# Gate products and pairs of short latent products in a fixed alternation, and the second rotary pair beside the latent heads: a two-layer encoder on one core

## The chip, the cores and the metric

The kernel runs on one core of one Trainium2 chip. The core has TensorE (PE in the profile, its weight loads PEld), VectorE (DVE), ScalarE (ACT), GpSimd (POOL) and SyncE (SP, which here issues nearly all loads), each with a queue of its own that it works through in order. The metric is the device time of one execution in microseconds (us), as the median of the runs shown.

## The reference

A bidirectional encoder of two layers over 256 tokens of width 2048, in float32. What matters here is the token mixer of each layer:

```python
h = rmsnorm(x, g_mix[i])
z = h @ w_in[i]
dq, dk, dv, cq, ckv, kr, ga, gb = jnp.split(z, split_at, axis=-1)
...
od = diff_attention(dq, dk, dv, lam)            # 8 heads, two softmax maps each
y_diff = od.reshape(b, s, DIFF_WIDTH) @ w_branch_diff[i]
qf = (rmsnorm(cq, g_q_latent[i]) @ w_q_up[i]).reshape(b, s, MLA_HEADS, MLA_NOPE_DIM + MLA_ROPE_DIM)
q_nope = qf[..., :MLA_NOPE_DIM]
q_rope = apply_rope(qf[..., MLA_NOPE_DIM:], cos_m, sin_m)
...
om = latent_attention(q_nope, q_rope, k_nope, k_rope, v_mla)   # 8 heads
y_mla = om.reshape(b, s, MLA_WIDTH) @ w_branch_mla[i]
merged = jax.nn.sigmoid(ga) * y_diff + jax.nn.sigmoid(gb) * y_mla
x = x + merged @ w_out[i]
```

A feed-forward part and a gated embedding follow in each layer; the change does not touch them.

## The kernel before

Activations are kept transposed, features on the 128 partitions and the 256 tokens along the free axis. Every operand of a product is a float32 value split into a high and a low part in a rounded format. Weights arrive in pieces of 128x1024 (512 KB). For each piece, SP issues the load into one of four w32 buffers (line 203), ACT copies it to the high part whi (line 204, three buffers) and DVE subtracts to get the low part wlo (lines 204 and 82, three buffers). This is `piece`; in this text the DVE subtraction is called the weight split.

A piece holds eight 128x128 tiles. `emit` spends two matmuls on each tile: whi against the activation's high and low part, 512 columns (line 254), and wlo against the high part, 256 columns (line 255). They go into one of four PSUM banks of the pool ps_mm, named mm. `joined` then adds the two halves of a bank: ACT copies one half to SBUF (line 279), DVE adds the other (line 82). That addition frees the bank.

Three kinds of product matter here. A *gate* (`gate`, line 632) has 16 tiles and so two pieces; its joined sum is multiplied by a row of norm factors and stored. A *plain pair* is `queries_up(n)` with n of 0, 2, 4 or 6: one piece of w_q_up makes two short products of four tiles each, one for each of two heads, and each is joined and split into high and low part again. A *rotary pair* is `queries_up(8)` or `queries_up(10)`: the same two short products, and then `rotated` turns each: a shuffle, two multiplications and an addition on DVE, then two half-height copies on ACT and two half-height splits on DVE for each product. queries_up(8) serves latent heads 0 to 3, queries_up(10) serves heads 4 to 7.

In each layer the eight heads of the differential attention run first, two steps of the generator `beside` in each head. `beside` makes the queries and keys of later heads, the latent keys (`keys_up`), the shared rotary key (`shared_key`, matmuls on line 409), and last the four pairs queries_up(8), (0), (2), (10) and four gates. After them come the values of the latent heads (`values`, w_v, lines 223 to 227), then the eight latent heads. Each latent head calls `some_gate` twice. That makes one gate, and ahead of it what the dictionary `later` names for that step: the normalisation and transposes of four differential heads (`settle`, transposes on line 693), queries_up(4) and queries_up(6). In between stand scores (line 437), transposes of the softmax weights (line 459) and the heads' outputs (lines 674 and 747).

The order of instructions on each engine is not that of the source alone. A scheduler orders them when the program is built, by its own times for them; `tc.issue_after` and `tc.add_manual_dep` with NO_SYNC force an order between two instructions without a wait. Engines wait for one another through semaphores.

Of the kernel before, what the change touches and what calls it, by code (L numbers as in the profile page):

```python
# [49 lines left out]
NO_SYNC = mybir.DependencyInfo(mybir.DependencyClass.NoSync, mybir.DependencyReason.DATA)  # L50
# [10 lines left out]
def encoder(ctx, tc, x, p, positions, cols, lams, wq, wk, wv, wcq, wckv, wkr, wga, wgb,  # L61
            w_q_up, w_kn, w_v, w_bd, w_bm, w_out, w_gate, w_up, w_down, w_pin, w_pg, w_pin_end, w_pg_end, g_end, rope_c, out):
    nc = tc.nc
    V, A, PE = nc.vector, nc.scalar, nc.tensor
# [13 lines left out]
    def bank(ps=ps_at, tag="at", name="at", shape=(P, 2 * T)):  # L78
        return ps.tile(list(shape), F32, tag=tag, name=name)

    def tt(o, a, b, op):
        return V.tensor_tensor(out=o, in0=a, in1=b, op=op)  # L82
# [17 lines left out]
    def operand(t):  # L100
        return t.rearrange("p c t -> p (c t)")
# [4 lines left out]
    def in_turn(u):  # L106
        return u.rearrange("p (c h t) -> p h t c", c=2, h=2)
# [21 lines left out]
    ones = const.tile([P, P], F32, name="ones")  # L129
# [103 lines left out]
            if j:  # L233
                tt(sq0[0], sq0[0], sq0[j], ALU.add)

    last_split, last_mm, chores, sq0, step, last_block = [], [], [], [], [], [None]

    def after_splits():

# [5 lines left out]
    def emit(acc, hi, lo, at, us, first, last, whole):  # L245
        for j, u in enumerate(us):
            s, start, stop = slice((at + j) * P, (at + j + 1) * P), first and j == 0, last and j == len(us) - 1
            t = in_turn(u)
            if whole:
                PE.matmul(acc[:, :T], hi[:, s], t[:, 0], start=start, stop=False)  # L250
                PE.matmul(acc[:, :T], hi[:, s], t[:, 1], start=False, stop=False)
                PE.matmul(acc[:, :T], lo[:, s], t[:, 0], start=False, stop=stop)
            else:
                PE.matmul(acc, hi[:, s], t, start=start, stop=False)  # L254
                last_block[0] = PE.matmul(acc[:, T:], lo[:, s], t[:, 0], start=False, stop=stop)  # L255

    def product(src, us, whole=False):
# [10 lines left out]
    def pair(src, us):  # L268

        n = len(us)  # L270
        hi, lo = piece(src.rearrange("n p m -> p n m"), 2 * n)
        for j in range(2):
            acc = bank(ps_mm, "mm", "mm")
            emit(acc, hi, lo, j * n, us, True, True, False)
            yield acc

    def joined(acc, o=None):
        t = scratch("join", 3)
        A.activation(t, acc[:, T:], AF.Copy)  # L279
        o = scratch("a", 4) if o is None else o  # L280
        tt(o, acc[:, :T], t, ALU.add)
        return o

    def split(u, src, gain=None, blocks=False):
        src = src.rearrange("p (c t) -> p c t", c=2) if blocks else by_parity(src)
        hi, lo = (parts(u)[:, j] for j in range(2))
        if gain is None:
            return A.activation(hi, src, AF.Copy), tt(lo, src, hi.bitcast(F32), ALU.subtract)  # L288
        return A.activation(hi, src, AF.Copy, scale=gain), stt(lo, src, gain, hi.bitcast(F32), ALU.mult, ALU.subtract)  # L289
# [96 lines left out]
    def rotated(a, c_, s_, o):  # L386
        turn(a, c_, s_)
        for j, q in enumerate(stacked(o)):
            own, other = (slice(64 * i, 64 * i + 64) for i in (j, 1 - j))
            A.activation(q[own], by_parity(a[own]), AF.Copy, scale=MLA_SCALE)  # L390
            stt(q[other], by_parity(a[own]), MLA_SCALE, q[own].bitcast(F32), ALU.mult, ALU.subtract)
# [4 lines left out]
    def shared_key(src, us, c_, s_):  # L396

        acc = bank(ps_mm, "mm", "mm")
        half = NC // 2
        for k in range(0, NC, half):  # L400
            w = wts.tile([P, PT * P], F32, tag="w32", name="wk32", bufs=W_BUFS)[:, : half * 64]
            both = wts.tile([P, PT * P], F32R, tag="whi", name="wkey", bufs=3)
            hi, lo = both.rearrange("p (k c n) -> p c k n", c=2, n=64)[:, 0], both.rearrange("p (k c n) -> p c k n", c=2, n=64)[:, 1]
            nc.sync.dma_start(w, src[:, k * 64 : (k + half) * 64])
            w = w.rearrange("p (k n) -> p k n", n=64)
            A.activation(hi, w, AF.Copy)
            tt(lo, w, hi.bitcast(F32), ALU.subtract)
            for j in range(half):
                PE.matmul(acc, both[:, j * P : (j + 1) * P], in_turn(us[k + j]), start=k + j == 0, stop=k + j == NC - 1)  # L409
        a, low = scratch("a", 4), slice(0, 64)  # L410
        base = acc[low, :T]
        for part in (acc[64:, :T], acc[low, T:]):
            t = scratch("join", 3)
            A.activation(t[low], part, AF.Copy)
            tt(a[low], base, t[low], ALU.add)
            base = a[low]
        A.activation(a[64:], a[low], AF.Copy)
        turn(a, c_, s_)
        for j, t in enumerate(krs):
            hi, lo = (parts(t)[:, i] for i in range(2))  # L420
            own = slice(64 * j, 64 * j + 64)
            A.activation(hi, by_parity(a), AF.Copy)
            tt(lo[own], by_parity(a[own]), hi[own].bitcast(F32), ALU.subtract)
# [103 lines left out]
    for L in range(DEPTH):  # L527
# [31 lines left out]
        def queries_keys(h):  # L559
            for which, w in enumerate((wq, wk)):  # L560
                a = joined(product(w[L, h], ua))
                sh = scratch("sh", 2)
                V.stream_shuffle(sh, a, ROPE16)
                tt(sh, sh, sr, ALU.mult)
                tt(a, a, cr, ALU.mult)
                tt(a, a, sh, ALU.add)
                split(qk[h][which], a, None if which else DIFF_SCALE)
# [17 lines left out]
        def keys_up(n):  # L585
            for acc in pair(w_kn[L, n : n + 2], ckv):
                kn.append(operand(fb(len(kn), F32R)))
                split(kn[-1], joined(acc))

        def queries_up(n):  # L590
            for acc in list(pair(w_q_up[L, n : n + 2], cq)):
                if n < MH:
                    qn.append(operand(fa(PLACES[len(qn)], F32R)))
                    split(qn[-1], joined(acc), MLA_SCALE)
                else:
                    if n > MH:
                        qr.append(operand(fc(len(qr) - 2, F32R)))
                    at = qr[len(qr) - 1] if n > MH else qr[ropes[0]]
                    rotated(joined(acc), cos_m, sin_m, at)
                    ropes[0] += 1  # L600
# [13 lines left out]
        def beside():  # L614

            for h in range(2, DH):
                queries_keys(h)
                yield
                if h < 6:
                    keys_up(2 * h - 4)  # L620
                elif h == 7:
                    shared_key(wkr[L], ua, crm, srm)
                yield
            for j, n in enumerate((8, 0, 2, 10)):
                queries_up(n)
                if j % 2:
                    gate(wga, gate_a, next(todo))
                yield
            for _ in range(2):
                gate(wga, gate_a, next(todo))  # L630

        def gate(w, store, n):
            tt(store(n), joined(product(w[L, n], ua)), R, ALU.mult)
# [12 lines left out]
        todo = iter(range(NC))  # L646
# [38 lines left out]
        def settle(h0):  # L685

            rd = rsqrt(ssd[:, 2 * h0 : 2 * h0 + 8], P, SUB_EPS, 8)
            for h in range(h0, h0 + 4):
                t = bank()
                for b in range(2):  # L690
                    o, j = od[h][:, b * P : (b + 1) * P], 2 * (h - h0) + b
                    ts(o, o, rd[:, j : j + 1], None, ALU.mult)
                    PE.transpose(t[:, b * P : (b + 1) * P], o, ident)  # L693
                split(ods[h], t[:, :T], gsub[:, L : L + 1], blocks=True)
# [17 lines left out]

        oms = ub[12:] + ub[8:12]
        ahead = iter(range(EARLY))
        later = {0: lambda: settle(0), 2: lambda: queries_up(4), 4: lambda: settle(4), 7: lambda: queries_up(6)}
        steps = itertools.count()

        def some_gate():
# [49 lines left out]
        acc, add = stream(ub, f"g_ffn{L}")  # L768
# [5 lines left out]
        R, _, pre = normed_rows(acc, lambda: product(w_gate[L, 0], ub), lambda: product(w_up[L, 0], ub))  # L774
# [5 lines left out]
        for part, (f0, f1) in enumerate(FF_PARTS):  # L780
            for f in range(f0, f1):
                a = pre.pop(0) if pre else joined(product(w_gate[L, f], ub))
                tt(a, a, R, ALU.mult)
                s = scratch("sig", 2)
# [7 lines left out]
            if last:  # L792
                acc, add = stream(ub, f"g_ple{L}")
# [8 lines left out]
            if part == 1 and L == DEPTH - 1:  # L802
# [7 lines left out]
                hi, lo = piece(w_pin_end, 8)  # L810
                for b in range(2):
                    acc_ = bank(ps_mm, "mm", "mmv")
                    for k in range(2):
                        s = slice(k * 512, (k + 1) * 512)
# [14 lines left out]
        else:  # L829
            acc, add = stream(ua, f"g_mix{L + 1}")  # L830
        for n in range(FM if final else NC):
            a = pre.pop(0) if pre else joined(product(w_pg[L * NC + n], ub))
            tt(a, a, R, ALU.mult)
            s = scratch("sig", 2)
# [4 lines left out]
            if final and n in (3, 5):  # L839
                b = (n - 3) // 2  # L840
                t = bank()
# [6 lines left out]
    for a in range(0, first, 2):  # L848
        m = min(2, first - a)
        hi, lo = piece(w_pg_end[:, a * 512 : (a + m) * 512], 4 * m)  # L850
        for j in range(m):
            s = slice(j * 512, (j + 1) * 512)
# [176 lines left out]
```

## Time and profile before

| what | value |
|---|---|
| runs | 2720.01, 2720.53 and 2720.7 us, median 2720.53 |
| the profiled execution's own time | 2720.81 us |
| its span, first to last instruction | 2719.0 us |
| granted TensorE clock, mean | 0.999 |
| share of the span on the chain that ended last | PE 98%, DVE 1% |
| ACT's weight copies (line 204) | x1024, 1030 ns each |
| DVE's weight splits (line 82, wlo) | x1024, 1189 ns each |
| SP's queue, share of 16 DMA engines | 60.5% |

Matmuls are pipelined and their ends are modelled, so the time that one takes from the engine is read from the distance of the starts of two neighbours, not from its duration. The same holds for DVE, where one instruction's end lies beside the next one's start. A row of the timeline gives the start, the duration, the engine, the line, the operation, output and inputs by their names, their shape and the number of instructions, and behind them in brackets the engine's idle time before it with what ended it. A row of the table by stretch gives the stretch and its length, then the busy time of PE, PEld, DVE, ACT and POOL, the granted clock, the share of the DMA engines that was busy and GB/s. The two layers run the same stages: the stretch that the change touches lies from about 184 to 330 us in layer 0 and from about 1534 to 1680 in layer 1.

### The profile page before, as it was taken

The page shows a single profiled execution, that of the slowest core. Times are in us where ns is not written, and L with a number is a line of the kernel's source. Part 1 is how long each engine was busy: PE and PEld are TensorE (multiplying, and loading weights), DVE is VectorE, ACT ScalarE, POOL GpSimd, SP SyncE. Part 2 cuts the span into 40 slices and gives each one's busy share as a digit, 9 for nine tenths or more (in the row PEclk, how much of TensorE's full clock was granted, in tenths as well). Part 3 has the DMA queues.
Part 4 walks back from the last instruction along what each step waited for, and adds up shares of the span by engine and source line. Part 5 has one row for each costly group of instructions (what it writes and reads, how often), then busy time and mean ns, then how long its engine had stood idle before and what let it go on. Part 6 is the DMA issues. An engine that isn't in the chain of part 4 may idle for free.

```text
span 2719.0 us, 43648 instructions
## 1 busy us (share of the span) xinstructions
PE 2706.3 (100%) x16608; PEld 2482.9 (91%) x16608; DVE 2064.6 (76%) x3426; ACT 1570.1 (58%) x2562; POOL 1.7 (0%) x9
## 2 busy tenths in 40 slices
PE   9999999999999999999999999999999999999998
PEld 8999999999999999999989899999999999999997
DVE  8899668777667777777869986687776677677777
ACT  7786557565445545555747865565554455455555
POOL 0000000000000000000000000000000000000000
PEclk9999999999999999999999999999999999999999
DMA  7555566666666666666665555666656666666665
GB/s 253 178 166 180 164 201 200 201 200 201 197 205 201 194 201 209 201 203 199 202 200 172 164 180 173 201 201 201 201 200 197 205 202 190 212 200 201 200 199 164
DMA packets 157058, 531.53 MB, mean 195 GB/s; under 512 B 17200, under 2 KB 23472, under 8 KB 156848
## 3 DMA queue, kind: packets, MB, share of 16 engines
q1 hardware_dynamic: 156272, 527.90, 60.5%
q8 instruction: 130, 2.13, 0.3%
q10 hardware_dynamic: 576, 0.85, 0.1%
q14 instruction: 80, 0.66, 0.1%
HBM read 526.58 MB, written 2.10 MB: 194 GB/s over the span
## 4 chain that ended last, share of the span: by engine, by line
PE 98%; DVE 1%; ACT 0%; issue 0%; DMA 0%; SPq 0%; ACTq 0%
PE mm L254 61%; PE mm L255 30%; PE mmv L223 1%; PE mmv L227 1%; PE mmv L226 1%; PE S L437 1%; PE at L459 1%; PE at L674 0%; PE at L747 0%; DVE wlo L82 0%; DVE a L82 0%; DMA w<-in_wv 0%; ACT whi L204 0%; PE at L693 0%; PE mm L409 0%
## 5 line engine op out<-in xcount | busy, mean ns | idle before, releaser
L204 ACT ACTIVATE whi<-w 128x1024 fp32r<-128x1024 f32 (+2 forms) x1024 | 1054.5, 1030 | 1070.0 <-issue 512.5
L82 DVE TENSOR_TENSOR wlo<-w,whi 128x1024 fp32r<-128x1024 f32 (+2 forms) x1024 | 1217.4, 1189 | 574.3 <-ACT whi L204 563.7
L254 PE MATMUL mm<-ub,whi 128*128 128x512 f32 x3904 | 1281.4, 382 | 3.2 <-DVE a L82 3.2
L254 PE MATMUL mm<-ua,whi 128*128 128x512 f32 x3704 | 1222.1, 383 | 0.0
L255 PE MATMUL mm<-ub,wlo 128*128 128x256 f32 x3904 | 1063.2, 273 | 0.0
L255 PE MATMUL mm<-ua,wlo 128*128 128x256 f32 x3704 | 1010.6, 273 | 0.0
L254 PEld LDWEIGHTS mm<-ub,whi 128*128 128x128 f32 x3904 | 737.6, 189 | 105.8 <-DVE a L82 3.8
L254 PEld LDWEIGHTS mm<-ua,whi 128*128 128x128 f32 x3704 | 699.6, 189 | 94.7
L255 PEld LDWEIGHTS mm<-ub,wlo 128*128 128x128 f32 x3904 | 749.5, 192 | 0.4
L255 PEld LDWEIGHTS mm<-ua,wlo 128*128 128x128 f32 x3704 | 711.0, 192 | 2.2 <-DVE wlo L82 0.6
L82 DVE TENSOR_TENSOR a<-mm,join 128x256 f32<-128x256 f32 x418 | 173.8, 417 | 0.1
L279 ACT ACTIVATE join<-mm 128x256 f32<-128x256 f32 x444 | 162.8, 368 | 4.2 <-PE mm L255 4.0
L82 DVE TENSOR_TENSOR xT<-xT,mm 128x256 f32<-128x256 f32 x256 | 106.8, 420 | 33.4 <-PE mm L255 29.3
L82 DVE TENSOR_TENSOR a<-a,row 128x256 f32<-128x256 f32 x204 | 86.1, 424 | 5.8
L288 ACT ACTIVATE ua<-a 128x256 fp32r<-128x256 f32 x120 | 59.1, 492 | 2.6 <-DVE a L82 2.6
L82 DVE TENSOR_TENSOR ua<-a,ua 128x256 fp32r<-128x256 f32 x120 | 55.0, 458 | 1.2 <-ACT ua L288 1.2
L82 DVE TENSOR_TENSOR a<-a 128x256 f32<-128x256 f32 x120 | 51.0, 425 | 4.0
L450 ACT ACTIVATE E<-S,nm 128x256 f32<-128x256 f32 x96 | 44.4, 476 | 12.8 <-DVE nm L448 12.3
L223 PE MATMUL mmv<-whi,ua 128*128 128x512 f32 x132 | 50.6, 384 | 0.4 <-ACT whi L204 0.4
L226 PE MATMUL mmv<-whi,ua 128*128 128x512 f32 x132 | 50.0, 380 | 0.0
L227 PE MATMUL mmv<-wlo,ua 128*128 128x512 f32 x132 | 43.7, 380 | 0.0
L289 ACT ACTIVATE ub<-xT,gcol 128x256 fp32r<-128x256 f32 x64 | 39.5, 618 | 1.7 <-DVE xT L82 1.7
(227 smaller groups left out, 1245.0 us busy)
## 6 DMA issues: line engine op xcount, KB each, us to landing
w<-in_w_gate SPq DMA_DIRECT2D x176, 512.0 KB, 4.7
w<-in_w_up SPq DMA_DIRECT2D x176, 512.0 KB, 4.7
w<-in_w_down SPq DMA_DIRECT2D x128, 512.0 KB, 4.3
w<-in_wga SPq DMA_DIRECT2D x64, 512.0 KB, 3.8
w<-in_wgb SPq DMA_DIRECT2D x64, 512.0 KB, 4.1
w<-in_w_out SPq DMA_DIRECT2D x64, 512.0 KB, 4.7
w<-in_w_pg SPq DMA_DIRECT2D x56, 512.0 KB, 4.7
w<-in_w_down SPq DMA_DIRECT2D x64, 384.0 KB, 3.8
```

The lines of the kernel that those rows point to most:

```text
L82: return V.tensor_tensor(out=o, in0=a, in1=b, op=op)
L204: last_split[:] = A.activation(hi, w, AF.Copy), tt(lo, w, hi.bitcast(F32), ALU.subtract)
L223: mm = PE.matmul(bank_, xh, wh, start=first, stop=False)
L226: PE.matmul(bank_, xl, wh, start=False, stop=False)
L227: return PE.matmul(bank_, xh, wl, start=False, stop=last)
L254: PE.matmul(acc, hi[:, s], t, start=start, stop=False)
L255: last_block[0] = PE.matmul(acc[:, T:], lo[:, s], t[:, 0], start=False, stop=stop)
L279: A.activation(t, acc[:, T:], AF.Copy)
L288: return A.activation(hi, src, AF.Copy), tt(lo, src, hi.bitcast(F32), ALU.subtract)
L289: return A.activation(hi, src, AF.Copy, scale=gain), stt(lo, src, gain, hi.bitcast(F32), ALU.mult, ALU.subtract)
L437: mm = PE.matmul(S[:, b, :], q[:, b], k, start=j == 0, stop=j == len(pairs) - 1)
L450: last_exp[0] = A.activation(E[:, b, :].rearrange("p (c t) -> p c t", c=2), by_parity(S[:, b, :]), AF.Exp, bias=nm[:, b : b + 1], accum_ou ...
```

## The change

The last four pairs and four gates of `beside` become gate, queries_up(8), gate, queries_up(0), gate, queries_up(2), gate. While they are written, a flag makes `emit` force the first matmul of each product to be issued behind the last matmul of the product written before it. queries_up(10) leaves `beside` and becomes step 3 of `later`, in the second half of latent head 1's turn.

```diff
-    last_split, last_mm, chores, sq0, step, last_block = [], [], [], [], [], [None]
+    last_split, last_mm, chores, sq0, step, last_block, in_order = [], [], [], [], [], [None], [False]
...
-                PE.matmul(acc, hi[:, s], t, start=start, stop=False)
+                mm = PE.matmul(acc, hi[:, s], t, start=start, stop=False)
+                if start and in_order[0]:
+                    tc.add_manual_dep(mm.ins, last_block[0].ins.name, NO_SYNC, reason="short products between long ones")
                 last_block[0] = PE.matmul(acc[:, T:], lo[:, s], t[:, 0], start=False, stop=stop)
...
-            for j, n in enumerate((8, 0, 2, 10)):
-                queries_up(n)
-                if j % 2:
-                    gate(wga, gate_a, next(todo))
-                yield
-            for _ in range(2):
-                gate(wga, gate_a, next(todo))
+            in_order[0] = True
+            gate(wga, gate_a, next(todo))
+            yield
+            queries_up(8)
+            gate(wga, gate_a, next(todo))
+            yield
+            queries_up(0)
+            yield
+            gate(wga, gate_a, next(todo))
+            queries_up(2)
+            yield
+            gate(wga, gate_a, next(todo))
+            in_order[0] = False
...
-        later = {0: lambda: settle(0), 2: lambda: queries_up(4), 4: lambda: settle(4), 7: lambda: queries_up(6)}
+        later = {0: lambda: settle(0), 2: lambda: queries_up(4), 3: lambda: queries_up(10), 4: lambda: settle(4), 7: lambda: queries_up(6)}
```

The program holds the same matmuls, loads and ACT and DVE operations as before, in another order. In the changed source the lines below `emit` stand two to eight further down.

*The loads on SyncE's queue behind the shared key, layer 0, before.* A load of in_w_q_up is a pair, two loads of in_wga are a gate, in_w_v are the values.

```order
L203 DMA w32_2367<-in_w_q_up 128x2x512
L203 DMA w32_2456<-in_w_q_up 128x2x512
L203 DMA w32_2496<-in_wga 128x1024
L203 DMA w32_2518<-in_wga 128x1024
L203 DMA w32_2556<-in_w_q_up 128x2x512
L203 DMA w32_2601<-in_w_q_up 128x2x512
L203 DMA w32_2654<-in_wga 128x1024
L203 DMA w32_2676<-in_wga 128x1024
```

The same place in the changed program:

```order
L203 DMA w32_2369<-in_wga 128x1024
L203 DMA w32_2391<-in_wga 128x1024
L203 DMA w32_2457<-in_w_q_up 128x2x512
L203 DMA w32_2508<-in_wga 128x1024
L203 DMA w32_2530<-in_wga 128x1024
L203 DMA w32_2568<-in_w_q_up 128x2x512
L203 DMA w32_2615<-in_wga 128x1024
L203 DMA w32_2637<-in_wga 128x1024
L203 DMA w32_2664<-in_w_q_up 128x2x512
L203 DMA w32_2713<-in_wga 128x1024
L203 DMA w32_2735<-in_wga 128x1024
L203 DMA w32_2765<-in_w_v 128x1024
```

Each pair now has a gate ahead of it and one behind it; the fourth pair is queued 20 loads behind the shared key's, where it was queued five behind.

*DVE before, in the same stretch of layer 0, where the first gate's bank mm_2495 is freed.* a, sh and join are buffers of a product on its way, ub14 and fa5 hold finished queries, E is a head's softmax weights, rsum its factors.

```order
L85 SCALAR_TENSOR_TENSOR ub14_106<-a_2393,ub14_106 64x256
L82 TENSOR_TENSOR sh_2408<-sh_2408,sin_m_579 128x256
L82 TENSOR_TENSOR a_2406<-a_2406,cos_m_578 128x256
L88 TENSOR_SCALAR rsum_2434<-rsum_2434,neg_lam_129 128x2
L85 SCALAR_TENSOR_TENSOR ub14_106<-a_2393,ub14_106 64x256
L82 TENSOR_TENSOR wlo_2655<-w32_2654,whi_2656 128x1024
L82 TENSOR_TENSOR a_2542<-mm_2495,join_2540 128x256
L85 SCALAR_TENSOR_TENSOR fa5_2487<-a_2490,fa5_2487 128x2x128
```

And on PE, the product that takes that bank, mm_2616, the second half of queries_up(0):

```order
L254 MATMUL mm_2607<-ub11_103,whi_2603 128x512
L255 MATMUL mm_2607<-ub11_103,wlo_2602 128x256
L254 MATMUL mm_2616<-ub8_100,whi_2603 128x512 [waits DVE_49]
L255 MATMUL mm_2616<-ub8_100,wlo_2602 128x256
L254 MATMUL mm_2616<-ub9_101,whi_2603 128x512
```

DVE in the changed program, where queries_up(0)'s weight split wlo_2569 stands. mm_2463 and mm_2472 are the two products of queries_up(8):

```order
L82 TENSOR_TENSOR a_2483<-mm_2463,join_2481 128x256
L383 STREAM_SHUFFLE sh_2485<-a_2483 128x256
L453 RECIPROCAL rsum_2435<-sm_2434 128x4
L82 TENSOR_TENSOR sh_2485<-sh_2485,sin_m_579 128x256
L82 TENSOR_TENSOR a_2483<-a_2483,cos_m_578 128x256
L88 TENSOR_SCALAR rsum_2435<-rsum_2435,neg_lam_129 128x2
L82 TENSOR_TENSOR a_2496<-mm_2472,join_2494 128x256
L82 TENSOR_TENSOR a_2483<-a_2483,sh_2485 128x256
L82 TENSOR_TENSOR wlo_2569<-w32_2568,whi_2570 128x1024
L383 STREAM_SHUFFLE sh_2498<-a_2496 128x256
```

And on PE, the first product of queries_up(0), mm_2574, behind the second gate, mm_2507, and a head's output:

```order
L254 MATMUL mm_2507<-ua15_91,whi_2532 128x512
L257 MATMUL mm_2507<-ua15_91,wlo_2531 128x256
L682 MATMUL at_2557<-vals_147,wt_2455 128x128 [waits Activation_49]
L682 MATMUL at_2557<-vals_147,wt_2455 128x128 x3
L254 MATMUL mm_2574<-ub8_100,whi_2570 128x512 [waits DVE_49,PE_49,Activation_49]
L257 MATMUL mm_2574<-ub8_100,wlo_2569 128x256 [waits DVE_49]
```

Before, three pairs of short products follow within two gates of one another and the rotary passes of queries_up(8) lie between them on DVE; now those passes lie beside the second gate.

*DVE beside the latent heads, layer 0, before*: the third head's softmax weights E and, between weight splits, the normalisation of the last four differential heads (ra, ry and the rows on fa2 and fa3).

```order
L88 TENSOR_SCALAR E_3154<-E_3154,rsum_3167 128x256 x2
L85 SCALAR_TENSOR_TENSOR ra_3248<-ry_3247 128x8
L82 TENSOR_TENSOR wlo_3313<-w32_3312,whi_3314 128x1024
L82 TENSOR_TENSOR ra_3248<-ra_3248,rv_3246 128x8
L85 SCALAR_TENSOR_TENSOR ry_3247<-ra_3248,ry_3247 128x8
L88 TENSOR_SCALAR fa2_2156<-fa2_2156,ry_3247 128x128 x4
L88 TENSOR_SCALAR fa3_2550<-fa3_2550,ry_3247 128x128 x4
L82 TENSOR_TENSOR wlo_3374<-w32_3373,whi_3375 128x1024
```

The same place in the changed program:

```order
L88 TENSOR_SCALAR E_3102<-E_3102,rsum_3115 128x256 x2
L82 TENSOR_TENSOR wlo_3291<-w32_3290,whi_3292 128x1024
L82 TENSOR_TENSOR sh_3164<-sh_3164,sin_m_579 128x256
L82 TENSOR_TENSOR a_3162<-a_3162,cos_m_578 128x256
L85 SCALAR_TENSOR_TENSOR ry_3247<-ra_3248,ry_3247 128x8
L82 TENSOR_TENSOR a_3176<-mm_3150,join_3174 128x256
L82 TENSOR_TENSOR a_3162<-a_3162,sh_3164 128x256
L85 SCALAR_TENSOR_TENSOR ra_3248<-ry_3247 128x8
L82 TENSOR_TENSOR wlo_3313<-w32_3312,whi_3314 128x1024
L383 STREAM_SHUFFLE sh_3178<-a_3176 128x256
L82 TENSOR_TENSOR ra_3248<-ra_3248,rv_3246 128x8
L85 SCALAR_TENSOR_TENSOR fc0_3159<-a_3162,fc0_3159 64x256 x2
```

The rotary passes of queries_up(10) (a_3162, a_3176, fc0) now stand between these weight splits, and the rows on fa2 and fa3 are moved behind them.

## The prediction

> **What bounds the kernel now.** I read the page first, then the view of waits for TensorE (PE), then the timelines of PE, VectorE (DVE) and ScalarE (ACT) around the waits found, then the table of busy times by stretch.
>
> ```profile
> span 2719.0 us, 43648 instructions
> PE 2706.3 (100%) x16608; PEld 2482.9 (91%) x16608; DVE 2064.6 (76%) x3426; ACT 1570.1 (58%) x2562; POOL 1.7 (0%) x9
> PE mm L254 <- DVE a L82: 3.2, 2, 1.6
> PE at L516 <- DVE share L135: 1.1, 1, 1.1
> PE mmv L223 <- ACT whi L204: 0.4, 1, 0.4
> ```
>
> PE is idle for 2719.0 - 2706.3 = 12.7 us of the span. The view of waits names 4.7 us of it: two waits of 1.6 us for a VectorE addition, and 1.5 us at the start of the program. No change inside the layers can gain more than PE's idle time there and what a restart costs, unless it takes matmuls away, and this one takes none. The two waits are the same place in layer 0 and layer 1:
>
> ```profile
> 202.10 0.27 PE L255 MATMUL mm<-ub,wlo 128*128 128x256 f32 x1
> 202.21 0.38 PE L254 MATMUL mm<-ub,whi 128*128 128x512 f32 x1
> 202.43 0.27 PE L255 MATMUL mm<-ub,wlo 128*128 128x256 f32 x1
> ...
> 205.70 0.27 PE L255 MATMUL mm<-ub,wlo 128*128 128x256 f32 x1
> 207.57 0.48 PE L254 MATMUL mm<-ub,whi 128*128 128x512 f32 x1 [1.60 <-DVE a L82]
> 207.90 0.27 PE L255 MATMUL mm<-ub,wlo 128*128 128x256 f32 x1
> ...
> 1555.96 0.27 PE L255 MATMUL mm<-ub,wlo 128*128 128x256 f32 x1
> 1557.84 0.48 PE L254 MATMUL mm<-ub,whi 128*128 128x512 f32 x1 [1.61 <-DVE a L82]
> 1558.16 0.27 PE L255 MATMUL mm<-ub,wlo 128*128 128x256 f32 x1
> ```
>
> The operand ub says that these are the short products of queries_up. Elsewhere one L254 and one L255 take 202.43 - 202.10 = 0.33 us from start to start. The wait stands before the eighth short product, mm_2616 in the order shown above, which needs the PSUM bank of the first gate product, mm_2495. Who is late, and why:
>
> ```profile
> 200.88 0.27 PE L255 MATMUL mm<-ua,wlo 128*128 128x256 f32 x1
> 205.95 0.41 ACT L279 ACTIVATE join<-mm 128x256 f32<-128x256 f32 x1
> 205.96 1.23 DVE L82 TENSOR_TENSOR wlo<-w,whi 128x1024 fp32r<-128x1024 f32 x1
> 207.10 0.42 DVE L82 TENSOR_TENSOR a<-mm,join 128x256 f32<-128x256 f32 x1
> 196.00:202.00 6.00, 6.00 (x41) 5.60 (x40) 6.00 (x13) 5.17 (x15) 0.00 (x0) 1.00 0.56 175
> 202.00:208.00 6.00, 4.40 (x27) 3.79 (x26) 5.86 (x16) 5.95 (x16) 0.00 (x0) 1.00 0.29 90
> 208.00:214.00 6.00, 6.00 (x40) 5.53 (x39) 5.91 (x12) 4.97 (x10) 0.00 (x0) 1.00 0.53 173
> ```
>
> The gate product ends at 201, ACT copies half of it only at 205.95, and DVE adds the other half at 207.10, behind a weight split. In the stretches (length, then PE, PEld, DVE, ACT, POOL, clock, DMA) DVE is busy 6.00 and 5.86 of 6 us and ACT 5.95. So **VectorE and ScalarE set the pace here**, and PE is idle 1.60 of 6. The transfers do not: DMA is busy 0.29.
>
> **The change part by part.** *The wait that goes.* PE loses 207.57 - 205.70 - 0.11 = 1.76 us, 0.11 being the spacing after an L255 (202.10 to 202.21). After it the first L254 takes 0.33 us to the next start in place of 0.22, 0.11 more. That is 1.87 us in layer 0. In layer 1, 1557.84 - 1555.96 - 0.11 + 0.10 = 1.87. Together 3.74 us.
>
> Where rows and a page differ: the restarted L254 has 0.48 us in place of 0.38. The Trainium skill, "TensorE: Matmul & The Clock Gate", section "Single matmul latency", gives a lone warm matmul of N columns (398 + N)/2.4 ns, which is 379 ns at 512, and its section "Back-to-back issue gap" N/2.4 + 2.5, which is 216 ns; a drained pipe would cost the difference, 0.16 us. By it the estimate is 1.60 + 0.16 = 1.76 us a layer and 3.5 us in all. The row of 0.48 us says that the page's 0.38 is not the whole of it here.
>
> *Does nothing take its place?* What DVE owes for each product, against what PE spends on it, comes from these rows:
>
> ```profile
> 201.15 1.22 DVE L82 TENSOR_TENSOR wlo<-w,whi 128x1024 fp32r<-128x1024 f32 x1
> 202.29 0.41 DVE L82 TENSOR_TENSOR a<-mm,join 128x256 f32<-128x256 f32 x1
> 198.93 1.28 DVE L448 TENSOR_REDUCE nm<-S 128x2 f32<-128x512 f32 x2
> 200.13 0.44 DVE L85 SCALAR_TENSOR_TENSOR fa<-a,fa 128x256 fp32r<-128x256 f32 x1
> 216.55 0.42 DVE L82 TENSOR_TENSOR sh<-sh,sin_m 128x256 f32<-128x256 f32 x1
> 216.88 0.43 DVE L82 TENSOR_TENSOR a<-a,cos_m 128x256 f32<-128x256 f32 x1
> 221.62 2.01 DVE L85 SCALAR_TENSOR_TENSOR fc<-a,fc 64x256 fp32r<-64x256 f32 x4
> 223.66 1.23 DVE L82 TENSOR_TENSOR wlo<-w,whi 128x1024 fp32r<-128x1024 f32 x1
> ```
>
> From start to start a weight split takes 1.14 us, a 128x256 pass 0.33, four half-height splits 2.04. A **gate** owes two weight splits, an addition and a multiplication: 2.9 us for 16 x 0.33 = 5.2 us of PE. A **plain pair** (queries_up(0), (2)) owes one split and four passes: about 2.5 for 8 x 0.33 = 2.6 of PE. A **rotary pair** (queries_up(8), (10)) owes one split, two additions, two shuffles, six passes and the four half-height splits: 1.14 + 10 x 0.33 + 2.04 = 6.5 for 2.6. Before: two pairs, a gate, two pairs, three gates. Now: gate, pair, gate, pair, gate, pair, gate; one rotary pair is gone from the stretch. DVE is relieved by 6.5 us, PE by 2.6 and the wait.
>
> The tightest place that I find in the new order is mm_2574, the first product of queries_up(0), with its weight split wlo_2569. PE reaches it after two gates, queries_up(8), two groups of L674 and one head's scores and transposes:
>
> ```profile
> 194.39 0.94 PE L437 MATMUL S<-fa,ub 64*128 64x256 f32 x12
> 195.67 0.46 PE L254 MATMUL mm<-ua,whi 128*128 128x512 f32 x1
> 200.99 1.06 PE L674 MATMUL at<-vals,wt 128*128 128x128 f32 x8
> 201.80 0.46 PE L254 MATMUL mm<-ub,whi 128*128 128x512 f32 x1
> 188.16 0.59 PE L254 MATMUL mm<-ub,whi 128*128 128x512 f32 x2
> 184.43 1.23 DVE L82 TENSOR_TENSOR wlo<-w,whi 128x1024 fp32r<-128x1024 f32 x1 [0.77 <-ACT whi L204]
> ```
>
> The stretch starts at 188.16 on PE and 184.43 on DVE in both orders. PE: 188.16 + 2 x 5.24 + 2.62 + 2 x 0.89 (200.99 to 201.80, and 0.08 in the L254 behind it) + 1.4 (194.39 to 195.67 with its two changes) = 204.4. DVE has, up to and with wlo_2569, six weight splits (6.8), two pairs of row maxima at 1.20 (2.4) and 28 smaller instructions at about 0.34 (9.5): 184.43 + 18.7 + about 0.4 idle = 203.5. It is there 0.9 us early. Behind it each gate lets DVE gain 5.2 - 2.9 = 2.3 us, so the margins grow. The addition that was late before, a gate's for a later short product, is now due 9 us or more after that gate (a pair, a gate and a group of L674 lie between: 2.6 + 5.2 + 0.9, and more); before, it was due after 4.8 and came after 6.4. Cost 0; bounds: nothing, to the whole old wait back (+3.7).
>
> *The forced order* on PE puts no instruction or semaphore of its own; a product that is not ready now holds back the one behind it, and behind that the scores of the next head. With DVE early it holds nothing: 0, bounds as above.
>
> *queries_up(10) beside the heads.* The same matmuls, one load of 512 KB and the same ACT and DVE work. On SyncE's queue its load is moved past 15 others. Four w32 buffers keep loads ahead of PE:
>
> ```profile
> DMA to landing us min/median/max: 3.2/3.5/4.5
> 256.00:262.00 6.00, 6.00 (x41) 5.58 (x40) 5.79 (x22) 3.51 (x9) 0.00 (x0) 1.00 0.35 117
> 262.00:268.00 6.00, 6.00 (x43) 5.60 (x43) 4.60 (x11) 3.25 (x7) 0.00 (x0) 1.00 0.59 182
> 268.00:274.00 6.00, 6.00 (x41) 5.53 (x40) 5.18 (x10) 3.27 (x9) 0.00 (x0) 1.00 0.44 156
> 274.00:280.00 6.00, 6.00 (x42) 5.58 (x40) 4.11 (x6) 3.39 (x6) 0.00 (x0) 1.00 0.56 175
> ```
>
> The load lands in 3.5 us, w_q_up's own median, while one gate is 5.2: hidden. DVE's spare time over 256 to 280 is 0.21 + 1.40 + 0.82 + 1.89 = 4.3 us, and the pair brings 2.6 us of PE: 6.9 against the 6.5 it owes. It fits, narrowly at first, and only its split and two additions (1.8 us) hold a buffer or a bank; the rotary passes are due for head 4, two heads later. I take 0; bounds 0 to 3.7 a layer (below).
>
> *Fewer changes of kind.* An L254 behind a group of transposes takes 0.30 to the next start (201.80 to 202.10) in place of 0.22. I count 22 such groups a layer from the shared key to the heads' end in the old order, 21 in the new: at 0.1 to 0.3 us with entry and exit, -0.2 for two layers; bounds 0 and -0.6.
>
> **Sum.** The profiled execution took 2720.81 us, its span and 1.8 around it. 2720.81 - 3.74 - 0.2 = 2716.9. It lies 0.3 above the median shown, 2720.53, from which the sum is 2716.6. I say **2716.7**.
>
> **The rivals.** *A. A smaller wait comes back* before wlo_2569 or a bank near it. For: DVE is at 6.00 of 6, and my margin of 0.9 us is the sum of 38 instructions and ignores ACT, busy 5.95 of 6. Against: ACT loses a rotary pair too. If DVE is 1.8 us later than I count, PE waits 0.9 a layer: 2718.7.
>
> *B. The wait only moves*, to another bank freed late: 1.87 a layer again, 2720.6. It decides if a gate's addition comes over 8.7 us after the gate.
>
> *C. Slower: the rotary pair starves the heads.* Its place is behind the third head's first transposes, at about 255 in the old times, and in 256 to 262 DVE has 0.21 spare. If all 6.5 us must be done within that stretch and the pair's own 2.6 of PE, PE waits 6.5 - 2.6 - 0.2 = 3.7 a layer, 2716.9 + 7.4 = 2724.3. It decides from the point where the rotary passes stand ahead of the next weight splits on DVE. Against: the new order puts the splits wlo_3291 and wlo_3313 between them. The Trainium skill, same page, Part 1, says that PE idle beyond about 3.4 us halves its clock; by it such a wait would cost up to 1.7 us more a layer. The wait of 1.60 here left it at 1.00.
>
> **How the numbers follow.** Forecast (2716.0 to 2717.6) 0.80; A 0.10; B 0.04; C 0.04; faster than all of them 0.02. The range runs from 2715.8, the switches' bound with some spread, to 2719.0, which holds A. A measurement of this kernel tells about 0.2%, 5.4 us, from no change: faster means under 2715.1, which the idle time nearly rules out (0.03); slower means over 2726.0, C at more than its price (0.03); within 0.2% 0.94.
>
> **What would show it.** Right: the view of waits has no PE wait for "DVE a L82"; PE's busy time differs from the span by about 9.5 us; around 196 to 215 DVE falls below 6.00 while PE stays full; from 250 to 280 DVE rises and PE stays full. Wrong: a PE wait on wlo or a bank around 204 (A, B), or around 255 to 270 (C); a wait that remains in only one layer would contradict my reading that both are one mechanism.

## The result and the profile after

The changed kernel takes 2716.70 us (median of 22 runs, 2716.14 to 2717.37); the kernel before, timed beside it, 2720.42 us (22 runs, 2719.74 to 2721.01). The ratio is 0.9986, 95% interval 0.9981 to 0.9992. The forecast was 2716.7 us. The difference of the medians, 3.72 us, agrees with the 3.74 us at which the prediction priced the two waits. One execution of the first experiment below (4758.81 us, granted clock 0.556) and one of the seventh (2867.09 us, 0.924) ran slower than the others and are left out of the ratios.

From the page and the view of waits for PE of the changed kernel:

```profile
span 2715.2 us, 43642 instructions
PE 2705.4 (100%) x16608; PEld 2485.2 (92%) x16608; DVE 2064.5 (76%) x3426; ACT 1570.4 (58%) x2562; POOL 1.7 (0%) x9
PE at L518 <- DVE share L135: 1.1, 1, 1.1
PE mmv L223 <- ACT whi L204: 0.7, 1, 0.7
```

The waits for "DVE a L82" are gone from both layers and no new one inside the layers is named. PE's span less its busy time is 9.8 us in place of 12.7. The table by stretches (length, then busy us of PE, PEld, DVE, ACT and POOL, clock, DMA) over the stage with the wait and the stage that took in queries_up(10):

```profile
196.00:202.00 6.00, 6.00 (x42) 5.46 (x41) 5.89 (x16) 4.97 (x16) 0.00 (x0) 1.00 0.49 171
202.00:208.00 6.00, 6.00 (x43) 5.63 (x42) 5.91 (x15) 5.77 (x14) 0.00 (x0) 1.00 0.35 114
208.00:214.00 6.00, 6.00 (x38) 5.54 (x37) 5.91 (x11) 5.09 (x10) 0.00 (x0) 1.00 0.66 218
...
256.00:262.00 6.00, 6.00 (x40) 5.58 (x39) 5.94 (x17) 4.04 (x7) 0.00 (x0) 1.00 0.54 175
262.00:268.00 6.00, 6.00 (x42) 5.61 (x41) 5.91 (x16) 3.47 (x5) 0.00 (x0) 1.00 0.52 167
268.00:274.00 6.00, 6.00 (x40) 5.53 (x39) 5.96 (x17) 4.03 (x9) 0.00 (x0) 1.00 0.45 154
274.00:280.00 6.00, 6.00 (x45) 5.66 (x44) 4.74 (x8) 3.34 (x5) 0.00 (x0) 1.00 0.60 197
```

PE is at 6.00 of 6 throughout. DVE is hardly less busy where the wait was (5.89, 5.91, 5.91), and from 256 to 280 it went from 5.79 + 4.60 + 5.18 + 4.11 = 19.7 to 22.6 us. DVE did not become free; only what PE asks of it falls due at other times. The timelines of DVE and PE show the two places that the prediction worked out:

```profile
202.79 1.22 DVE L82 TENSOR_TENSOR wlo<-w,whi 128x1024 fp32r<-128x1024 f32 x1
209.04 0.42 DVE L82 TENSOR_TENSOR a<-mm,join 128x256 f32<-128x256 f32 x1
...
204.45 0.46 PE L254 MATMUL mm<-ub,whi 128*128 128x512 f32 x1
204.75 0.27 PE L257 MATMUL mm<-ub,wlo 128*128 128x256 f32 x1
212.82 0.38 PE L254 MATMUL mm<-ub,whi 128*128 128x512 f32 x1
```

The split wlo_2569 ends at 204.01, 0.44 us before PE comes to the product that reads it and 0.74 us before the first matmul on the low part (L257, 204.75). The second gate's addition ends at 209.46; its bank is asked for at 212.82, four products later.

### The profile page after: what moved, and what is told of

It is laid out like the page before. It is cut to its first block, busy times and chain, and to the rows that moved or that the text cites. A ratio compares the mean times of both kernels' runs of the same rounds, so it can differ in the third digit from the quotient of the medians.

```text
span 2715.2 us, 43642 instructions
## 1 busy us (share of the span) xinstructions
PE 2705.4 (100%) x16608; PEld 2485.2 (92%) x16608; DVE 2064.5 (76%) x3426; ACT 1570.4 (58%) x2562; POOL 1.7 (0%) x9
## 4 chain that ended last, share of the span: by engine, by line
PE 99%; ACT 0%; DMA 0%; SPq 0%; issue 0%; DVE 0%; ACTq 0%
PE mm L254 61%; PE mm L257 31%; PE mmv L227 1%; PE mmv L223 1%; PE mmv L226 1%; PE S L439 1%; PE at L461 1%; PE at L682 1%; PE at L755 0%; PE mm L411 0%; DMA w<-in_wv 0%; PE at L701 0%; PE at L317 0%; PE at L324 0%; ACT L890 0%; ACT fb L938 0%
## 5 line engine op out<-in xcount | busy, mean ns | idle before, releaser
L82 DVE TENSOR_TENSOR wlo<-w,whi 128x1024 fp32r<-128x1024 f32 (+2 forms) x1024 | 1218.1, 1190 | 569.3 <-ACT whi L204 559.1
L257 PE MATMUL mm<-ub,wlo 128*128 128x256 f32 x3904 | 1064.8, 273 | 0.0
L257 PE MATMUL mm<-ua,wlo 128*128 128x256 f32 x3704 | 1011.1, 273 | 0.0
L257 PEld LDWEIGHTS mm<-ub,wlo 128*128 128x128 f32 x3904 | 750.7, 192 | 0.3
L257 PEld LDWEIGHTS mm<-ua,wlo 128*128 128x128 f32 x3704 | 712.2, 192 | 2.1 <-DVE wlo L82 0.6
L82 DVE TENSOR_TENSOR a<-mm,join 128x256 f32<-128x256 f32 x418 | 174.2, 418 | 0.1
L82 DVE TENSOR_TENSOR xT<-xT,mm 128x256 f32<-128x256 f32 x256 | 106.8, 420 | 33.4 <-PE mm L257 29.3
L82 DVE TENSOR_TENSOR a<-a,row 128x256 f32<-128x256 f32 x204 | 86.2, 424 | 5.8
L82 DVE TENSOR_TENSOR ua<-a,ua 128x256 fp32r<-128x256 f32 x120 | 54.7, 455 | 1.2 <-ACT ua L290 1.2
L82 DVE TENSOR_TENSOR a<-a 128x256 f32<-128x256 f32 x120 | 50.9, 424 | 4.0
```

## The experiments

Three theories were tested. **1, reuse of the bank**: four banks go round, so PE asks for a gate's bank again when three further products are done; behind a gate the old order put three short ones (3.9 us), the new one a pair and a gate (7.8). The three short ones are queries_up(2) and the first half of queries_up(10); mm_2616, the product that waited, is the second half of queries_up(10) and not of queries_up(0), since its weights are the fourth load of in_w_q_up, w32_2601. **2, debt**: DVE owes the whole stretch too much, and the second rotary pair had to leave it. **3**: the forced order on PE carries the gain. Theory 4, ACT, came with the fourth run. The 95% intervals of the single experiments (given behind each ratio) reach about 2.4 us to each side; smaller differences between them rest on the waits in the traces.

**The alternation alone.** queries_up(10) stays in `beside`.

```diff
             gate(wga, gate_a, next(todo))
+            queries_up(10)
             in_order[0] = False
-        later = {..., 3: lambda: queries_up(10), ...}
+        later = {...}
```

> The alternation alone: the forced order of gates and pairs of the change, but queries_up(10) stays beside the diff heads, behind the fourth gate, as in the kernel before. Theory 1 (the wait stood on one bank of one gate, whose addition was late on DVE because short products followed that gate too closely): the alternation alone takes the wait away, and what the second rotary pair owes falls due only for latent head 4, so 2716.7 us (2716.2 to 2717.4). Theory 2 (the stretch as a whole owes DVE too much, and the pair of 6.5 us DVE for 2.6 us PE has to leave it): the gain comes back as a wait behind the fourth gate, where DVE of the changed kernel has 0.66 + 0.64 + 0.20 = 1.5 us spare from 214 to 232; 6.5 - 2.6 - 1.5 = 2.4 us a layer, so about 2721 us.

Measured: 2716.60 us (ratio 0.9986, 0.9977 to 0.9995), no wait inside the layers. The alternation gives the whole gain with the pair still in the stretch.

**The move alone**, in the old order.

```diff
-                queries_up(n)
+                if n < 10:
+                    queries_up(n)
```

with step 3 of `later` as in the change.

> The move alone: queries_up(10) beside the latent heads at step 3, everything else in the order of the kernel before (pair, pair, gate, pair, then three gates, no forced order). Theory 1: the bank of the first gate is now asked for only after a pair and a whole gate (2.6 + 5.2 us) in place of one pair and a half, and its addition came 6.4 us after the gate, so the wait goes: 2716.7 us (2716.2 to 2717.6; the second gate's weight splits, at 205.96 in the old trace, may leave a wait of a few tenths). Theory 3 (the forced alternation is what removes the wait; without it two pairs still stand back to back): 1.87 us a layer stays, 2720.4 us.

Measured: 2717.72 us (0.9991, 0.9982 to 1.0), 0.1 us above theory 1's range. The bank's wait is gone, and a smaller one, 0.3 us a layer, stands before the second gate's second weight split (view of waits, then DVE's and PE's timeline):

```profile
PE mm L255 <- DVE wlo L82: 0.6, 2, 0.3
...
209.11 1.22 DVE L82 TENSOR_TENSOR wlo<-w,whi 128x1024 fp32r<-128x1024 f32 x1
...
210.38 0.38 PE L255 MATMUL mm<-ua,wlo 128*128 128x256 f32 x1 [0.32 <-DVE wlo L82]
```

So the move alone takes 2.7 of the 3.7 us, by theory 1's way (a gate now follows the pair behind the gate), and leaves DVE late for the next row.

**The change without the forced order.**

```diff
-            in_order[0] = True
+            in_order[0] = False
```

> The changed kernel without the forced order: in each of the three pairs the first matmul of the second short product stands right behind the first matmul of the first one, 0.9 us earlier on PE than with the forced order; all else is the same. Theory 1: four banks are there and each pair's second bank has been free for a gate's length by then, so the forced order is worth nothing: 2716.7 us (within 0.4 of the changed kernel). Theory 3 (the forced order carries the gain): waits of up to 0.9 us at each pair, 3 pairs, 2 layers, up to 2722 us.

Measured: 2716.68 us (0.9987, 0.9978 to 0.9995). The forced order is worth nothing here; theory 3 falls.

**The kernel before with DVE relieved.**

```diff
     def rotated(a, c_, s_, o, plain=False):
-        turn(a, c_, s_)
+        if not plain:
+            turn(a, c_, s_)
...
-                    rotated(joined(acc), cos_m, sin_m, at)
+                    rotated(joined(acc), cos_m, sin_m, at, n == MH)
```

> The kernel before, with its order, but the two products of queries_up(8) are not rotated (the shuffle, the two multiplications and the addition are left out, so latent heads 0 to 3 get unrotated queries): DVE owes 2 x 4 x 0.34 = 2.7 us less ahead of the wait, ACT and PE the same work. Theory 1 (DVE's backlog sets the time of the addition that frees the bank): the wait of 1.6 us goes, 2716.7 us (2716.4 to 2717.4). Theory 4 (ACT, busy 5.95 of 6 us there, sets it): DVE's relief does not help, the wait stays within 0.3 of 1.6 us a layer, 2720 us or more.

Measured: 2719.59 us (0.9997, 0.9988 to 1.0006). This fits neither expectation: only 0.84 of 3.74 us came off, and the named wait fell from 1.60 to 0.92 us a layer. DVE's and ACT's timelines of this run:

```profile
204.12 0.94 DVE L82 TENSOR_TENSOR kr<-a,kr 64x256 fp32r<-64x256 f32 x2
205.09 0.88 DVE L85 SCALAR_TENSOR_TENSOR E<-E,rsum,E 128x256 f32<-128x256 f32 x2
205.88 1.22 DVE L82 TENSOR_TENSOR wlo<-w,whi 128x1024 fp32r<-128x1024 f32 x1
207.02 0.75 DVE L82 TENSOR_TENSOR a<-mm,join 128x256 f32<-128x256 f32 x2
...
205.25 0.37 ACT L279 ACTIVATE join<-mm 128x256 f32<-128x256 f32 x1
```

The first gate's addition comes at 207.02, against 207.10 with 2.7 us more work: the order of DVE was made anew, and rows that nobody waits for yet (kr) or that stood behind the addition before (E) took the freed time. The copy of ACT is there at 205.62; the addition stands behind a weight split all the same.

**Two rows of DVE exchanged** in the kernel before: the addition ahead of that split.

```diff
         last_split[:] = A.activation(hi, w, AF.Copy), tt(lo, w, hi.bitcast(F32), ALU.subtract)
+        if behind[0] is not None:
+            tc.add_manual_dep(last_split[1].ins, behind[0].ins.name, NO_SYNC, ...)
+            behind[0] = None
```

(`behind[0]` is the first gate's addition, set only for the second gate's first piece.)

> The kernel before with one pair of rows exchanged on DVE: the addition of the first gate (a_2542, 207.10 in the old trace) stands ahead of the second gate's first weight split (wlo_2655, 205.96) and no longer behind it; PE's order and all other work are the same. If the wait is a bank that is held by a place in DVE's order (theory 1), the addition comes 1.14 us earlier and so does the matmul behind it: the wait falls from 1.6 to about 0.5 us a layer, 2720.4 - 2 x 1.14 = 2718.1 us (2717.6 to 2718.6). If DVE's whole debt in the stretch sets PE's pace (theory 2), an exchange of two rows gains nothing: the split is later by 0.33 us, and PE waits as long as before for it or for another bank, 2720.4 us.

Measured: 2721.09 us (1.0003, 0.9994 to 1.0012). PE's and DVE's timelines (the edit moves the lines of `emit`: here L257 is the matmul on whi, L258 the one on wlo):

```profile
205.85 0.48 PE L257 MATMUL mm<-ub,whi 128*128 128x512 f32 x1 [0.47 <-DVE a L82]
208.09 0.33 PE L462 MATMUL at<-ident,E 128*128 128x128 f32 x1 [0.67 <-DVE E L85]
208.82 0.55 PE L462 MATMUL at<-ident,E 128*128 128x128 f32 x3 [0.40 <-DVE E L85]
...
205.37 0.42 DVE L82 TENSOR_TENSOR a<-mm,join 128x256 f32<-128x256 f32 x1
207.56 0.48 DVE L85 SCALAR_TENSOR_TENSOR E<-E,rsum,E 128x256 f32<-128x256 f32 x1
207.95 0.42 DVE L82 TENSOR_TENSOR fc<-a,row 128x256 f32<-128x256 f32 x1
208.29 0.48 DVE L85 SCALAR_TENSOR_TENSOR E<-E,rsum,E 128x256 f32<-128x256 f32 x1
```

The bank's wait fell from 1.60 to 0.47 us, as theory 1 had it, and the time did not: behind that product the next head's transposes wait 0.67 + 0.40 us for E. The time is near theory 2's 2720.4, held by another row than the bank's. More than two rows moved, too: the gate's multiplication (207.95) came forward with the addition and now stands between the two rows of E. In the old order more than one row of DVE was late; the bank's was the first. Theory 1 alone was too simple for the old order.

**The wait brought back** in the changed kernel, by two pairs back to back behind a gate.

```diff
             queries_up(0)
             yield
-            gate(wga, gate_a, next(todo))
             queries_up(2)
             yield
+            gate(wga, gate_a, next(todo))
             gate(wga, gate_a, next(todo))
```

> The changed kernel, but queries_up(0) and queries_up(2) stand back to back behind the second gate, and the third and fourth gate behind them: the fourth product after the second gate is then a short one again and follows after 0.9 + 3 x 1.31 + 0.35 = 5.2 us, as before the change, in place of more than 7.9. DVE owes the same in all. Theory 1 (time from a gate to the reuse of its bank): in the changed kernel the second gate's addition ends at 209.4 and PE would ask for the bank at about 208.8, so 0.6 us and 0.1 for the restart come back in each layer: 2718.1 us (2717.4 to 2718.8). Theory 2 (what DVE owes in the stretch): it is relieved of the rotary pair as in the changed kernel, so 2716.7 us.

Measured: 2718.27 us (0.9992, 0.9984 to 1.0001), as theory 1 had it. View of waits, PE's and DVE's timeline:

```profile
PE mm L254 <- DVE a L82: 0.9, 2, 0.5
...
203.90 0.46 PE L254 MATMUL mm<-ub,whi 128*128 128x512 f32 x1
209.01 0.48 PE L254 MATMUL mm<-ub,whi 128*128 128x512 f32 x1 [0.51 <-DVE a L82]
...
208.54 0.42 DVE L82 TENSOR_TENSOR a<-mm,join 128x256 f32<-128x256 f32 x1
```

The addition ends at 208.96, and the fourth product behind that gate starts at 209.01. Counted from the first product behind the gate (203.90 here, 204.45 in the changed kernel), the addition ends after 5.06 us here and after 5.01 there: DVE is as late in both, and only the date has moved. The same work, with the rotary pair gone from the stretch, has a wait of the old kind again, about a third as long, because the distance is short again.

**More work for DVE** in the changed kernel.

```diff
+                    a = joined(acc)
+                    for _ in range(4 if n == MH else 0):
+                        ts(a, a, 1.0, None, ALU.mult)
-                    rotated(joined(acc), cos_m, sin_m, at)
+                    rotated(a, cos_m, sin_m, at)
```

> The changed kernel with four more passes of DVE over each of the two products of queries_up(8) (a multiplication by 1), 8 x 0.33 = 2.7 us more of DVE in the stretch. In the changed kernel the split wlo_2569 is done 0.66 us before the matmul that reads it. Theory 1 (only splits and the additions that free banks have a date; rotary passes are due much later and the order puts them behind): in this kernel's order wlo_2577, the same split, has one more pass ahead of it and the next one three more, so margins shrink by 0.3 and 1.0 us and PE waits 0 to 0.3 us a layer: 2716.7 to 2717.3 us. Theory 2 (the stretch's debt): 2.7 - 0.66 = 2.0 us a layer, 2720.8 us.

Measured: 2716.60 us (0.9987, 0.9978 to 0.9995), no wait. The passes were cheaper than expected:

```profile
200.94 0.68 DVE L88 TENSOR_SCALAR a<-a 128x256 f32<-128x256 f32 x3
201.54 1.22 DVE L82 TENSOR_TENSOR wlo<-w,whi 128x1024 fp32r<-128x1024 f32 x1
...
203.53 0.46 PE L254 MATMUL mm<-ub,whi 128*128 128x512 f32 x1
```

Three take 201.54 - 200.94 = 0.60 us, so the eight add 1.6 us and not 2.7. By theory 2 that still had to cost 1.6 - 0.74 = 0.9 us a layer (0.74 and not the expectation's 0.66 is the margin to the matmul that reads the split), 2718.5 us; it cost nothing. The passes did not all go behind the split: five of the eight stand ahead of it, three of them in the row shown. But the four rotary passes that stood ahead of it in the changed kernel now stand behind it, 4 x 0.33 us against 5 x 0.20, so it ends at 202.76, 0.77 us before its product at 203.53 (0.44 in the changed kernel). So the run shows that such work can be taken up without a wait when the order changes with it; it does not show what the passes would cost if the other rows kept their places.

**A gate behind each pair**, and nothing else changed in the kernel before.

```diff
                 queries_up(n)
-                if j % 2:
-                    gate(wga, gate_a, next(todo))
+                gate(wga, gate_a, next(todo))
                 yield
-            for _ in range(2):
-                gate(wga, gate_a, next(todo))
```

> The kernel before with nothing but the two last gates moved: pair (8), gate, pair (0), gate, pair (2), gate, pair (10), gate; the second rotary pair stays, and there is no forced order. Every gate's bank is asked for again only after a pair and a gate (2.6 + 5.2 us). Theory 1: the wait goes, 2716.7 us (2716.2 to 2717.4). Theory 2: the debt of two rotary pairs in the stretch is the same as before, the wait stays or moves to a weight split, 2718.5 us or more.

Measured: 2716.35 us (2716.08 to 2716.58; 0.9986, 0.9977 to 0.9994). Theory 2 falls: DVE owes the stretch all that it owed before the change. This is the smallest edit with the whole gain; that it is 0.35 us below the changed kernel is less than this measurement tells apart.

**The rotary pair late.** queries_up(10) at step 6 of `later`, the last before its reader, in place of 3.

> The changed kernel with queries_up(10) at step 6 of the latent heads in place of step 3, the last place ahead of head 4, which reads it. On PE some 10 us lie between the pair and the scores of head 4 that read fc0 (a gate of 5.2, a queries_up(6) of 2.6, transposes and products of a head); by then DVE owes about 4 us for that product, 2.9 for the gate, 1.1 for a split and the head's own 2 to 3. Theory 1 (the pair has time until it is read): 0 to 1 us a layer, 2716.7 to 2718.7 us. The prediction's rival C (the rotary pair starves the heads): 3.7 us a layer, 2724 us.

Measured: 2716.54 us (0.9986, 0.9977 to 0.9994). In two stretches behind the pair DVE is nearly full and PE is not held:

```profile
274.00:280.00 6.00, 6.00 (x43) 5.63 (x42) 5.91 (x16) 4.56 (x9) 0.00 (x0) 1.00 0.52 165
280.00:286.00 6.00, 6.00 (x41) 5.58 (x40) 5.91 (x11) 4.76 (x9) 0.00 (x0) 1.00 0.31 107
```

**ACT relieved, and both relieved**, in the kernel before. The edit, alone and on top of the unrotated queries_up(8):

```diff
             for b in range(2):
-                A.activation(E[0][:, b, :], E[0][:, b, :], AF.Copy, scale=r[0][:, b : b + 1])
                 stt(E[0][:, b, :], E[1][:, b, :], r[1][:, b : b + 1], E[0][:, b, :], ALU.mult, ALU.add)
```

> The kernel before without ACT's multiplication of the first half of a diff head's weights by 1/sum (two ACT instructions of 0.40 us a head, all diff heads; their output is left unscaled). DVE and PE have the same work. If DVE alone sets the time of the late addition, nothing changes: wait 1.6 us a layer, 2720.2 to 2720.6 us. If ACT sets it too, the addition comes up to 0.8 us earlier: 2718.8 to 2720 us.

> The kernel before with both relieved: queries_up(8) is not rotated (DVE -2.7 us), and ACT's multiplication of the diff heads' weights by 1/sum is left out (ACT -0.8 us a head). With DVE alone relieved a wait of 0.9 us stayed, ACT running without a gap from 197.6 to 211.6. If ACT is the second limit there, its 0.8 us come off what stayed: wait 0 to 0.2 us a layer, 2716.6 to 2717.5 us. If it is not (something in the order alone keeps the addition late), the wait stays at 0.9 a layer, 2719.6 us.

Measured: 2720.40 us alone (1.0, 0.9991 to 1.0009), a wait of 1.44 us; 2718.85 us with both (0.9994, 0.9986 to 1.0003), a wait of 0.71 us. The second lies between its two expectations. ACT alone does not set the wait; with DVE lighter its relief is worth 2719.59 - 2718.85 = 0.74 us, of which the named wait, 0.92 to 0.71 us a layer, shows 0.4. What stays is the order. From DVE's, ACT's and PE's timeline with both relieved:

```profile
204.77 1.23 DVE L82 TENSOR_TENSOR wlo<-w,whi 128x1024 fp32r<-128x1024 f32 x1
205.92 0.42 DVE L82 TENSOR_TENSOR a<-mm,join 128x256 f32<-128x256 f32 x1
...
203.69 0.37 ACT L279 ACTIVATE join<-mm 128x256 f32<-128x256 f32 x1
...
206.39 0.48 PE L254 MATMUL mm<-ub,whi 128*128 128x512 f32 x1 [0.71 <-DVE a L82]
```

The addition could have run at 204.77 and stands behind a weight split.

**The two edits that failed alone, together**: queries_up(8) unrotated and the addition ahead of the split.

> Both edits to the kernel before that failed alone: queries_up(8) is not rotated (DVE -2.7 us), and the first gate's addition stands ahead of the second gate's first weight split on DVE. PE keeps the old order of products. If the old wait is made of both, a place in DVE's order and DVE's debt behind it (first the addition is late, and with it early the rows that follow it), then neither suffices alone and both do: the addition comes at about 206.0 in place of 207.0, PE asks for the bank at about 206.5 behind the head's transposes, and the split behind it (done at about 207.4) is read at 207.9: no wait, 2716.7 us (2716.3 to 2717.3). If something else in the old order holds PE (a third row, or ACT), a wait of 0.5 us or more a layer stays, 2718 us or more.

Measured: 2717.95 us (0.9991, 0.9982 to 1.0), 1.2 us above the first expectation and close to the second, that something else holds PE. The view of waits names none inside the layers; the starts show where the time goes (L257 is again the matmul on whi, L258 the one on wlo):

```profile
205.40 0.27 PE L258 MATMUL mm<-ub,wlo 128*128 128x256 f32 x1
205.59 0.85 PE L463 MATMUL at<-ident,E 128*128 128x128 f32 x4
206.24 0.48 PE L257 MATMUL mm<-ub,whi 128*128 128x512 f32 x1
207.54 0.27 PE L258 MATMUL mm<-ub,wlo 128*128 128x256 f32 x1
207.70 0.48 PE L257 MATMUL mm<-ua,whi 128*128 128x512 f32 x1
208.02 0.27 PE L258 MATMUL mm<-ua,wlo 128*128 128x256 f32 x1
...
204.97 0.88 DVE L85 SCALAR_TENSOR_TENSOR E<-E,rsum,E 128x256 f32<-128x256 f32 x2
207.23 0.42 DVE L82 TENSOR_TENSOR a<-mm,join 128x256 f32<-128x256 f32 x1
```

From the last matmul ahead of the head's transposes to the next product it is 0.84 us, where the changed kernel has 0.46 (207.04 to 207.50): E ends at 205.85, and of the four transposes the second starts only at 205.90. The second gate then starts at 207.70, 0.16 us behind the matmul ahead of it in place of 0.11, and its first matmul takes 0.32 us to the next start in place of 0.22, as after a wait. It starts 0.05 us behind an addition that ends at 207.65, the distance that the waits named above have too (208.96 to 209.01), so the likely cause is a bank that comes a little late. Together that is about 0.5 us of the 0.6 us a layer. Both edits together win 2.5 of 3.7 us without touching PE's order; no run takes these last delays away one by one.

## Why the prediction was right, point by point

- **The wait that goes**, 3.74 us: right. It went in both layers, and 3.72 us between the medians agrees with its size. The interval of the ratio reaches 1.5 us to each side, so the result does not tell 3.74 from the prediction's other estimate, 3.5.
- **The number**: the sum gave 2716.6 from one start and 2716.9 from the other, with a term of -0.2 us that was not seen. That 2716.7 was met to the tenth is luck.
- **Who is late**: in part misread. The ACT row at 205.95 is the copy for queries_up(2); the gate's own copy is an earlier row of the old trace, ACT's timeline:

```profile
204.23 0.36 ACT L279 ACTIVATE join<-mm 128x256 f32<-128x256 f32 x1
```

  It had been ready for 2.5 us when DVE added at 207.10. "VectorE and ScalarE set the pace" should have been: DVE's order sets it, and ACT alone does not (2720.40 with ACT lighter). The sum did not rest on it.
- **Does nothing take its place**: right, with a smaller margin. wlo_2569 was forecast for 203.5 against PE at 204.4, 0.9 us; it was 204.01 against 204.45, 0.44 us (0.74 us to the matmul that reads the split). "Behind it the margins grow" by 2.3 us a gate was wrong: the next splits end some 1.2 us early, since DVE fills gained time with rotary passes. That also makes the margin robust: with 1.6 us of extra passes 0.77 us were left.
- **The bank of a gate**, due 9 us after the gate: right. The second gate ends on PE at about 203.8 and its bank is asked for at 212.8. This was the term that decided: shorten it, and 0.51 us of wait are back.
- **"DVE is relieved by 6.5 us"**: true, and not needed. The alternation has the whole gain without it.
- **queries_up(10) beside the heads**, 0: right, but "narrowly" was not. DVE is nearly full there (5.94, 5.91 and 5.96 of 6 us), but PE waits for none of it. It costs nothing three steps later either: in that run DVE finishes the first product at 279.46 and PE reads it at 281.98, so the date that rival C feared was far off.
- **The forced order**, 0: right, shown by leaving it out.
- **Fewer changes of kind**, -0.2 us: not seen. 3.72 measured against 3.74 for the waits alone leaves no room for more than a few tenths, and the runs of one kernel spread by more than that.

Shown: with DVE as late as it is here, a short distance from a gate to the reuse of its bank makes the wait, and the alternation removes it by distance. Not settled: how DVE and ACT share the rest of the lateness in the old order, since each relief also changed the order of the rows.

## What to carry to other kernels

Where accumulators go round a few banks, ask for each product how long PE works on the products in between before it wants the bank back, and set long ones between short ones; that cost nothing here, while taking 2.7 us of work a layer from the late engine won 0.8 us in all. An engine that runs its rows in a fixed order can have a row late by its place in that order, and not by its load alone: before removing work, look at which row stands ahead of the one that is waited for, and at what will be late next. Wherever a wait is removed, follow PE for some microseconds behind it, as the exchange of two rows shows.

## What the runs showed of the hardware

A pass of DVE over 128x256 with one input and a constant takes 0.20 us from start to start (0.60 us for three), one with two inputs 0.33 us; the expectation had taken them as equal. With a factor read from a buffer in place of the constant it is 0.27 us (two rows on E from 230.88 to 231.41 in the changed kernel). The Trainium skill, "VectorE: DVE Perf Modes", section "What auto-detection actually checks", says that an operation with a single source runs two elements at a time where source and destination lie in SBUF and their dimensions allow it, and that one with two sources does not for this type; the rows agree in kind, with a ratio of 0.33 / 0.20 = 1.65 and not 2. And the view of waits does not name every loss: in the last run it names none inside the layers, with 1.2 us lost to several short delays, which only the starts show.
